# DeltaNet layer: meta-token products stacked in float32r, decay matrices against a constant operand, K's norms off a diagonal, and the last down pairs block by block

## Chip, cores and metric

The kernel runs on one core of a Trainium2 chip, as one launch. The metric is the device time of one execution in microseconds (us); lower is better. Engines: PE is TensorE (matmul), PEld its weight loads, DVE VectorE, ACT ScalarE, POOL GpSimd, SP SyncE. A "q" behind an engine's name is its instruction queue.

## The reference

A trunk of two layers over 16 learned meta tokens and 512 real tokens, of 1024 features: multi-scale retention, a SwiGLU feed-forward net (FFN), gated DeltaNet, a second FFN, and a last RMSNorm that drops the meta tokens. All in float32. The change lies in the DeltaNet layer and at the end of the last FFN. DeltaNet, cut to what matters (8 heads, keys of 128, values of 256; chunks of 64 with the meta tokens in a chunk of their own):

```python
qkv = silu(causal_conv(h @ w_qkv, conv_w));  beta = sigmoid(h @ w_beta)
g = -exp(a_log) * softplus(h @ w_a + dt_bias)
q = l2norm(q) * DK ** -0.5;  k = l2norm(k)          # l2norm: x * rsqrt(sum(x*x) + 1e-6)
def step(state, inp):                                # per chunk
    gam = cumsum(gc);  decay = exp(where(i >= j, gam_i - gam_j, -inf))
    a_mat = where(i > j, beta * (k @ k.T) * decay, 0)
    u, w = solve(eye + a_mat, [v * beta, k * beta * exp(gam)])
    v_new = u - w @ state
    o = (q * exp(gam)) @ state + ((q @ k.T) * decay) @ v_new
    state = state * exp(gam_last) + (k * exp(gam_last - gam)).T @ v_new
o = gated_head_norm(o, norm_w, gate) @ w_out
h = h + (silu(h @ w_gate) * (h @ w_up)) @ w_down     # the FFN behind it
```

## The kernel before

Tokens are kept as 16 + 512 columns (T = 528, two halves of HH = 264); the kernel works in chunks of 128 real tokens and one of the 16 meta tokens. A float32 product of the projections is done as three float32r products (`mm3`): both operands are split into a rounded part and the rest (`hi`, `lo`; `split`), and hi.hi, hi.lo and lo.hi are summed in PSUM. Weights come by DMA (`wraw`), ACT rounds them (`whi`, L171) and DVE makes the rest (`wlo`, L172); there are three buffers of whi and wlo. A few small products use plain float32; each of them is two matmul instructions in the profile. A gemm of a projection is 8 x 3 x 2 products of 264 columns into a PSUM tile `g` (two buffers); smaller products share four PSUM tiles `m`.

The stages of the DeltaNet layer: `dn_gates` computes beta and g (48 products of 16 rows, `wh`/`wl` as the fixed operand, tiles kh and kl), their cumulated sums, and for each head the decay matrix of its four chunks: DVE multiplies the constant mask `later` by g (L1173), PE multiplies that by `tri` (L1180), ACT takes the exponent (L1182), POOL masks it with `tri` (L1183), a DMA stores it in d_dec. `dn_keys` runs two gemms per head (K is s = 0, Q is s = 1): PSUM is scaled into `pad` by DVE (L1057), the convolution is one ACT and three DVE operations (L1060, L1062), then silu (L1065) and the split `z` (L404, L405). `dn_norms` transposes K or Q on PE (L1211) and sums squares on ACT with an accumulated output (L1215), for the meta tokens too (L1220, L1222). `dn_attention` makes cc = beta / (norm + eps) and two other factors from it on DVE and POOL, then K.[K Q] for each chunk (12 products of 256 columns), scales the result by cc and the decay (L1254), and does the meta tokens' K.K (L1266, L1267). `dn_inverse` inverts the 32x32 blocks of all heads at once on DVE; `dn_merge` builds larger blocks on PE (L1330, L1360); `dn_by_token` transposes V; `dn_states` scans over the chunks for two heads at a time, and begins with the meta tokens: um.v0 (L1416), then kw.(that) gives the first state (L1425). Then `ffn1`: its second half of the down projection sums 22 x 128 hidden rows into four PSUM tiles, one for a block of 128 tokens; only the last pair of weight tiles is done block by block, and `add`, sum of squares, power on POOL, scaling and output DMA of a block follow (L1660 to L1678).

What sets the order: these stages are generators that are advanced in turn while gemms run (`spawn`, `tick`, `finish`, with constants such as NORMS, ATTEND and HOP that say after how many steps one is due), and a scheduler that then orders each engine's instructions. An engine's queue is fixed and is run in order: an instruction that waits holds up all behind it.

Of the kernel before, what the change touches and what calls it, by code (L numbers as in the profile page):

```python
# [48 lines left out]
HOP = 1.6  # L49


class Hybrid:
# [1015 lines left out]
    def dn_gates(self, sp, x, rb):  # L1068
# [23 lines left out]
        ba = self.t(self.tp, [P, T], "ra", bufs=4)[:16]
        nc.vector.tensor_tensor(self.halves(ba), p[:16, :, :HH], self.halves(rb[:16, :]), op=ALU.mult)
        yield GATE_STEPS[0]
        pt = self.psum_m()
        for ch in range(5):
            c0 = 0 if ch == 0 else NM + (ch - 1) * P
            nc.tensor.transpose(pt[:, ch * 16 : ch * 16 + 16], ba[:, c0 : c0 + P], self.ident[:16, :16])
        bt = self.t(gp, [P, 5, 16], "bt_")
        nc.scalar.copy(bt, pt[:, :80].rearrange("p (a b) -> p a b", b=16))  # L1100
        S = [P, 5, DH]
        beta, ax = self.t(gp, S, "beta"), self.t(gp, S, "ax_")
# [37 lines left out]
        for dst, mat in ((self.eglast, self.ones), (self.ekw, self.later)):  # L1140
# [3 lines left out]
            mm(pg[:, :DH], mat[:NM, :], gf[:NM, :DH], start=True, stop=True)  # L1144
# [4 lines left out]
        glm = self.um  # L1149
        S = [NM, DH, NM]  # L1150
        nc.vector.tensor_tensor(
# [16 lines left out]
        )  # L1168
        for hd in range(DH):
            yield 1  # L1170
            pd = self.psum_m()
            gls = self.t(sp, [P, 4, P], "vs", bufs=4)
            nc.vector.tensor_tensor(  # L1173
                gls,
                self.later.unsqueeze(1).to_broadcast([P, 4, P]),
                g[:, 1:, hd : hd + 1].to_broadcast([P, 4, P]),
                op=ALU.mult,
            )
            for ch in range(4):
                nc.tensor.matmul(pd[:, ch * P : (ch + 1) * P], gls[:, ch, :], self.tri, start=True, stop=True)  # L1180
# [5 lines left out]
    def dn_keys(self, pool, hd, x, rb, first, gt):  # L1186
# [5 lines left out]
        for s, base in ((1, 0), (0, 8)):  # L1192
# [10 lines left out]
            norms.append(self.spawn(self.dn_norms(hd, s, t_), NORMS))  # L1203
        return self.spawn(self.dn_attention(pool, hd, zh, zl, norms, gt), ATTEND)

    def dn_norms(self, hd, s, t_):
        nc = self.nc
        ssk = self.ssk[:, hd, :]
        pt = self.psum_m()
        for c in range(4):  # L1210
            nc.tensor.transpose(pt[:, c * P : (c + 1) * P], t_[:, NM + c * P : NM + (c + 1) * P], self.ident)  # L1211
        for c in range(4):
            jk = self.t(self.sp, [P, P], "rh")
            dst = ssk[:, c + 1 : c + 2] if s == 0 else self.eq[:, hd, c : c + 1]
            nc.scalar.activation(jk, pt[:, c * P : (c + 1) * P], AF.Square, accum_out=dst)  # L1215
        if s == 0:
            nc.vector.tensor_copy(self.kmf[:, hd, :], t_[:, :NM])
            yield 1
            pt = self.psum_m()
# [595 lines left out]
```

## Time and profile before

| | us |
|---|---|
| median of three runs | 1714.14 (1713.79 to 1717.31) |
| the profiled execution, whole | 1718.1 |
| its span, first to last instruction | 1716.3 |
| PE, DVE, ACT, POOL busy | 1687.9, 1193.9, 854.8, 89.1 |
| mean granted clock of TensorE | 0.994 |
| gates | from 819 to 839.5 |
| decay matrices of the eight heads, and the first head's attention | from 839.5 to 859.5 |
| keys, norms and attention of the eight heads | from 859.5 to 954.5 |
| inverse | from 954.5 to 1021 |
| scans in four pairs | from 1021 to 1330 |
| second FFN and output | from 1330 on |

Each profile row of an engine gives start and duration in us, engine, line, operation, output<-inputs by the program's names, and the form. A matmul's duration is the time from its start to its modelled end; since matmuls are pipelined, the distance between two starts is what one costs. In brackets stands the idle time before, and what ended it. Rows of groups by line end in busy time, mean ns of one, and idle time before them.

### The profile page before, as it was taken

The page shows a single profiled execution, that of the slowest core. Times are in us where ns is not written, and L with a number is a line of the kernel's source. Part 1 is how long each engine was busy: PE and PEld are TensorE (multiplying, and loading weights), DVE is VectorE, ACT ScalarE, POOL GpSimd, SP SyncE. Part 2 cuts the span into 40 slices and gives each one's busy share as a digit, 9 for nine tenths or more (in the row PEclk, how much of TensorE's full clock was granted, in tenths as well). Part 3 has the DMA queues.
Part 4 walks back from the last instruction along what each step waited for, and adds up shares of the span by engine and source line. Part 5 has one row for each costly group of instructions (what it writes and reads, how often), then busy time and mean ns, then how long its engine had stood idle before and what let it go on. Part 6 is the DMA issues. An engine that isn't in the chain of part 4 may idle for free.

```text
span 1716.3 us, 30519 instructions
## 1 busy us (share of the span) xinstructions
PE 1687.9 (98%) x12455; PEld 1575.2 (92%) x12455; DVE 1193.9 (70%) x1848; ACT 854.8 (50%) x1532; POOL 89.1 (5%) x148
## 2 busy tenths in 40 slices
PE   9999999999999999999999999999999999999997
PEld 9999999999999999999899988797977889999886
DVE  7786877754698887433788767685858798887322
ACT  5445555532445555322665437675656554545322
POOL 1000000000000000000210001010101000000010
PEclk9999999999999999999999999999999999999999
DMA  5554746562223333323264472333322222333221
GB/s 205 161 168 117 214 109 191 173 212 87 100 85 105 105 99 93 92 91 98 99 207 156 130 208 67 124 104 108 106 100 73 96 88 99 102 108 109 88 99 49
DMA packets 87116, 207.16 MB, mean 121 GB/s; under 512 B 20176, under 2 KB 37760, under 8 KB 85696
## 3 DMA queue, kind: packets, MB, share of 16 engines
q1 hardware_dynamic: 77056, 193.13, 33.7%
q0 software_dynamic: 2960, 10.24, 3.4%
q10 hardware_dynamic: 6960, 1.84, 0.5%
q8 instruction: 98, 1.61, 0.4%
q14 instruction: 42, 0.34, 0.1%
HBM read 180.85 MB, written 24.33 MB: 120 GB/s over the span
## 4 chain that ended last, share of the span: by engine, by line
PE 69%; DVE 8%; issue 5%; ACT 2%; POOL 1%; DMA 0%; ACTq 0%; POOLq 0%; DVEq 0%
PE g L414 54%; PE m L414 11%; DVE wlo L405 1%; DVE ra L1062 1%; DVE wlo L172 1%; DVE wsum L212 1%; POOL ss L1475 0%; ACT whi L404 0%; DVE flt L405 0%; PE m L1211 0%; PE m L1387 0%; DVE flb L405 0%; DMA wraw<-in_w_ret_dram 0%; ACT whi L171 0%; PE m L1330 0%
## 5 line engine op out<-in xcount | busy, mean ns | idle before, releaser
L172 DVE TENSOR_TENSOR wlo<-wraw,whi 128x1024 fp32r<-128x1024 f32 (+1 forms) x140 | 166.3, 1190 | 182.7 <-ACT whi L171 180.7
L171 ACT CAST whi<-wraw 128x1024 fp32r<-128x1024 f32 (+1 forms) x140 | 143.3, 1024 | 274.1 <-PE g L414 155.1
L414 PE MATMUL g<-xhi,whi 128*128 128x264 f32 (+1 forms) x1024 | 255.6, 314 | 2.5 <-DVE ra L775 2.4
L414 PE MATMUL g<-fht,whi 128*128 128x264 f32 (+1 forms) x912 | 256.6, 286 | 0.0
L414 PE MATMUL g<-fht,wlo 128*128 128x264 f32 (+1 forms) x912 | 254.9, 284 | 0.8 <-DVE wlo L405 0.8
L414 PE MATMUL g<-flt,whi 128*128 128x264 f32 (+1 forms) x912 | 254.4, 283 | 0.0
L414 PE MATMUL g<-xhi,wlo 128*128 128x264 f32 (+1 forms) x1024 | 249.9, 309 | 2.0 <-DVE wlo L172 2.0
L414 PE MATMUL g<-xlo,whi 128*128 128x264 f32 (+1 forms) x1024 | 249.3, 308 | 0.3 <-DVE xlo L468 0.3
L404 ACT CAST whi<-wraw 128x1024 fp32r<-128x1024 f32 x129 | 135.5, 1051 | 127.8 <-issue 51.3
L405 DVE TENSOR_TENSOR wlo<-wraw,whi 128x1024 fp32r<-128x1024 f32 x129 | 157.3, 1220 | 32.2 <-ACT whi L404 31.6
L414 PEld LDWEIGHTS g<-xhi,whi 128*128 128x128 f32 x1024 | 167.9, 191 | 12.6 <-DVE ra L775 2.6
L414 PEld LDWEIGHTS g<-xhi,wlo 128*128 128x128 f32 x1024 | 167.9, 191 | 10.7 <-DVE wlo L172 2.2
L414 PEld LDWEIGHTS g<-xlo,whi 128*128 128x128 f32 x1024 | 167.6, 190 | 7.4 <-DVE xlo L468 0.7
L414 PEld LDWEIGHTS g<-flt,whi 128*128 128x128 f32 x912 | 170.7, 189 | 0.2
L414 PEld LDWEIGHTS g<-fht,wlo 128*128 128x128 f32 x912 | 169.7, 188 | 1.0 <-DVE wlo L405 1.0
L414 PEld LDWEIGHTS g<-fht,whi 128*128 128x128 f32 x912 | 170.1, 188 | 0.4 <-ACT whi L404 0.2
L414 PE MATMUL g<-fhb,whi 128*128 128x264 f32 (+1 forms) x480 | 134.1, 288 | 0.0
L414 PE MATMUL g<-fhb,wlo 128*128 128x264 f32 (+1 forms) x480 | 132.6, 284 | 0.6 <-DVE wlo L405 0.5
L414 PE MATMUL g<-flb,whi 128*128 128x264 f32 (+1 forms) x480 | 132.0, 283 | 0.0
L405 DVE TENSOR_TENSOR wlo<-wsum,whi 128x1024 fp32r<-128x1024 f32 x54 | 66.1, 1225 | 44.3 <-ACT whi L404 44.3
L414 PEld LDWEIGHTS g<-fhb,wlo 128*128 128x128 f32 x480 | 88.5, 188 | 1.0 <-DVE wlo L405 1.0
L414 PEld LDWEIGHTS g<-flb,whi 128*128 128x128 f32 x480 | 89.1, 189 | 0.1
(445 smaller groups left out, 3769.9 us busy)
## 6 DMA issues: line engine op xcount, KB each, us to landing
wraw<-in_w_gu_dram SPq DMA_DIRECT2D x66, 512.0 KB, 3.2
wraw<-in_w_ret_dram SPq DMA_DIRECT2D x56, 512.0 KB, 4.1
wraw<-in_w_d_dram SPq DMA_DIRECT2D x38, 512.0 KB, 3.4
sraw<-in_w_gu_dram SPq DMA_DIRECT2D x22, 512.0 KB, 3.5
wraw<-in_w_ret_dram POOLq DMA_DIRECT2D x18, 512.0 KB, 5.5
wraw<-in_w_ro_dram SPq DMA_DIRECT2D x16, 512.0 KB, 3.5
wraw<-in_w_dqk_dram SPq DMA_DIRECT2D x16, 512.0 KB, 3.3
wraw<-in_w_dv_dram SPq DMA_DIRECT2D x16, 512.0 KB, 4.1
```

What stands on the lines that cost most here:

```text
L171: nc.scalar.copy(hi[:, c], raw[:, c])
L172: nc.vector.tensor_tensor(lo[:, c], raw[:, c], hi[:, c].bitcast(F32), op=ALU.subtract)
L212: nc.vector.scalar_tensor_tensor(dst[:, k, :], hh[:, kb + k, cs], g[:, kb + k : kb + k + 1], rb[:, cs], op0=ALU.mult, op1=ALU.mult)
L404: self.nc.scalar.copy(hi, src)
L405: self.nc.vector.tensor_tensor(lo, src, hi.bitcast(F32), op=ALU.subtract)
L414: mm(o, l, r[which], start=first and n == 0, stop=last and n == 2, **kw)
L1062: nc.vector.scalar_tensor_tensor(acc, pad[:, i : i + T], cw[:, mt, i : i + 1], acc, op0=ALU.mult, op1=ALU.add)
```

## The change

Line numbers in this section are those of the changed kernel.

**Gates.** hi and lo of w_ba lie in one fixed operand of 48 columns (rows 0 to 15 and 32 to 47 of the result), so two products with x's hi and lo replace three, 32 in place of 48. The five transposes become products against `pick`, which also adds the two parts. The meta tokens' values are spread to three copies, 32 rows apart.

**Decay matrices.** The mask `tri` is multiplied by g's hi and lo parts (two DVE products per head, L1194) and the constant `after` is the fixed operand of two 512-wide float32r products (L1200), where before four 128x128 float32 products had `tri` as the other operand.

**K's norms.** `dn_norms` is left for Q alone. For K, `diagonal` takes the sums of squares from the diagonal of K.K, which attention makes anyway: DVE multiplies a 128x128 block in PSUM by the identity and writes the accumulated sum (L1257), five times per head (one block of 96x96 for the meta tokens). cc and what follows come only after them, so the PSUM tiles of both chunk pairs and of the meta tokens are held until then.

**Meta products.** For um.v0 and kw.wm the meta tokens stand three times, 32 rows apart, as hi, hi and lo of one operand against hi, lo and hi of the other, so that one float32r product of 96 rows gives the three terms (L1461, L1474); DVE spreads and subtracts (L1464, L1469, L1418), and um is loaded by three DMAs and split (L1345).

**Tail.** `LAST = 2`: in the second half the last two pairs of down weights are held and done block by block.

The diff, cut to what the text speaks of:

```diff
+        wst = self.t(sp, [P, KT, 48], "zl", F32R, bufs=3)
+        nc.gpsimd.memset(wst.bitcast(F32), 0.0)
+        self.split(wst[:, :, 0:16], wst[:, :, 32:48], wr)
...
+            for i in range(2):
+                for half in range(2):
+                    nc.tensor.matmul(
+                        p[:48, half, :HH],
+                        wst[:, kt, :],
+                        x[i][:, kt, half * HH : half * HH + HH],
+                        start=kt == 0 and i == 0,
+                        stop=kt == KT - 1 and i == 1,
+                    )
...
+        after = self.t(sp, [P, P], "kh", F32R)
+        nc.scalar.copy(after, self.later)
+        g2 = self.t(sp, [P, 2, n5], "kl", F32R)
+        self.split(g2[:, 0, :], g2[:, 1, :], gf)
+        g2 = g2.rearrange("p t (a b) -> p t a b", b=DH).bitcast(F32)
...
-            gls = self.t(sp, [P, 4, P], "vs", bufs=4)
-            nc.vector.tensor_tensor(
-                gls,
...
-            )
-            for ch in range(4):
-                nc.tensor.matmul(pd[:, ch * P : (ch + 1) * P], gls[:, ch, :], self.tri, start=True, stop=True)
+            upto = self.t(sp, [P, 2, 4, P], "vs", F32R, bufs=4)
+            for i in range(2):
+                nc.vector.tensor_tensor(
+                    upto[:, i],
+                    self.tri.unsqueeze(1).to_broadcast([P, 4, P]),
+                    g2[:, i, 1:, hd : hd + 1].to_broadcast([P, 4, P]),
+                    op=ALU.mult,
+                )
+                nc.tensor.matmul(pd, after, upto[:, i].rearrange("p a b -> p (a b)"), start=i == 0, stop=i == 1)
...
-            norms.append(self.spawn(self.dn_norms(hd, s, t_), NORMS))
+            if s == 0:
+                nc.vector.tensor_copy(self.kmf[:, hd, :], t_[:, :NM])
+            else:
+                norms.append(self.spawn(self.dn_norms(hd, t_), NORMS))
...
+        def diagonal(dst, ps):
+            n = ps.shape[1]
+            jk = self.t(self.sp, [P, P], "rh")
+            nc.vector.scalar_tensor_tensor(
+                jk[:n, :n], ps, 1.0, self.ident[:n, :n], op0=ALU.mult, op1=ALU.mult, accum_out=dst
+            )
+
+        pk = self.psum_m()
+        self.spread(self.km, self.kmf[:, hd, :])
+        nc.tensor.matmul(pk[:96, :96], self.km, self.km, start=True, stop=True)
+        diagonal(ssk[:96, 0:1], pk[:96, :96])
+        ps = []
...
+                diagonal(ssk[:, c + 1 : c + 2], ps[cp][:, ci * 256 : ci * 256 + P])
+        nc.vector.tensor_scalar(irk, ssk, EPS, None, op0=ALU.add)
+        nc.vector.reciprocal(cc, irk)
+        nc.vector.tensor_tensor(cc, cc, self.beta[:, :, hd], op=ALU.mult)
+        for c in range(4):
...
-        km = self.kmf[:, hd, :]
-        nc.tensor.matmul(ps[:NM, :NM], km, km, start=True, stop=True)
         nc.vector.scalar_tensor_tensor(
-            self.mtm[:, hd, :], ps[:NM, :NM], cc[:NM, 0:1], self.decm0[:, hd, :], op0=ALU.mult, op1=ALU.mult
+            self.decm0[:, hd, :], pk[:NM, :NM], cc[:NM, 0:1], self.decm0[:, hd, :], op0=ALU.mult, op1=ALU.mult
...
+        for b in range(3):
+            (nc.sync, nc.scalar)[b % 2].dma_start(um[32 * b : 32 * b + NM], self.d_m1)
+        nc.scalar.copy(self.um, um)
+        nc.vector.tensor_tensor(self.um[64:96], um[64:96], self.um[64:96].bitcast(F32), op=ALU.subtract)
...
+        v0 = self.t(sp, [96, 256], "v0", F32R, bufs=4)
         irk = self.irk[:, hd, :]
+        vm = self.vm
+        for i in range(2):
+            self.spread(vm[:, i, :], va[i][:, :NM])
...
+        nc.vector.scalar_tensor_tensor(
+            v0[32:64], pt[32:64, :256], irk[32:64, 0:1], v0[32:64].bitcast(F32), op0=ALU.mult, op1=ALU.subtract
+        )
...
+        u3 = self.u3[hd % 2]
+        self.spread(u3, self.um[:, hd, :])
+        self.spread(self.km, self.kmf[:, hd, :])
         ps = self.psum_m()
-        mm(ps[:NM, :256], self.um[:, hd, :], vs[:NM, 0, :], start=True, stop=True)
-        wm = self.t(sp, [P, 256], "rr")
-        nc.scalar.copy(wm[:NM, :], ps[:NM, :256])
-        ps = self.psum_m()
-        nc.tensor.transpose(ps[:NM, :P], self.kmf[:, hd, :], self.ident)
-        kw = self.t(sp, [P, P], "kwf")
-        nc.scalar.activation(kw[:NM, :], ps[:NM, :P], AF.Copy, scale=self.kws[:NM, hd, 0:1])
+        mm(ps[:96, :256], u3, v0, start=True, stop=True)
+        wm = self.t(sp, [P, 256], "rh", F32R)
+        nc.scalar.copy(wm[:96], ps[:96, :256])
+        nc.vector.tensor_tensor(wm[32:64], ps[32:64, :256], wm[32:64].bitcast(F32), op=ALU.subtract)
...
+        nc.vector.scalar_tensor_tensor(
+            kw[64:96], kt_[64:96], kws[64:96], kw[64:96].bitcast(F32), op0=ALU.mult, op1=ALU.subtract
+        )
         yield
         ps = self.psum_m()
-        mm(ps[:, :256], kw[:NM, :], wm[:NM, :], start=True, stop=True)
+        mm(ps[:, :256], kw[:96], wm[:96], start=True, stop=True)
...
+            held = []
+            apart = LAST if half else 1
...
+                held.append((kp, self.load_w(a["w_d1"][half, kp])))
+                steps = [(k, i, b, w) for k, w in held for i in range(2) for b in range(4)]
+                if kp >= FT // 2 - apart:
+                    if len(held) < apart:
+                        continue
+                    steps.sort(key=lambda s: s[2])
+                held = []
+                for k, i, b, w in steps:
+                    kt, bs = 2 * k + i, slice(b * P, (b + 1) * P)
...
```

Where it moves instructions, at three places.

PE, decay burst, before. The tiles m are PSUM, one for each head, vs the products of L1173; g_9615 is a gemm of the key phase. The heads stand in one piece (the eighth follows):

```order
L414 MATMUL g_9615<-xhi_7750,whi_9611 128x264
L1160 MATMUL m_9426<-tri_471,um_9035 16x16 x8
L1180 MATMUL m_9437<-tri_471,vs_9438 128x128 x4
L1180 MATMUL m_9448<-tri_471,vs_9449 128x128 x4
L1180 MATMUL m_9459<-tri_471,vs_9460 128x128 x4
L1180 MATMUL m_9470<-tri_471,vs_9471 128x128 x4
L1180 MATMUL m_9481<-tri_471,vs_9482 128x128 x4
L1180 MATMUL m_9492<-tri_471,vs_9493 128x128 x4
L1180 MATMUL m_9503<-tri_471,vs_9504 128x128 x4
```

PE at the same place, after (kh is the constant `after`, vs one product of L1194; g_9604 and g_9685 are gemms, whi and wlo their weights):

```order
L1200 MATMUL m_9426<-vs_9427,kh_9421 128x512
L415 MATMUL g_9604<-xhi_7750,whi_9600 128x264
L415 MATMUL g_9604<-xlo_7751,whi_9600 128x264 x2
L1200 MATMUL m_9426<-vs_9427,kh_9421 128x512
L415 MATMUL g_9604<-xhi_7750,wlo_9601 128x264 x2
L415 MATMUL g_9685<-xhi_7750,whi_9681 128x264
L1200 MATMUL m_9436<-vs_9437,kh_9421 128x512
L415 MATMUL g_9685<-xhi_7750,whi_9681 128x264
L415 MATMUL g_9685<-xlo_7751,whi_9681 128x264 x2
L1200 MATMUL m_9436<-vs_9437,kh_9421 128x512
```

The products of the eight heads no longer stand together: up to the last of the sixteen, two rows with three gemm products lie between two of them.

DVE, key phase, before. The gemms' PSUM tiles follow each other on PE as g_9615, g_9695, g_9812, g_9892; pad takes one out, wlo_9889 is a weight tile of g_9892:

```order
L1057 TENSOR_TENSOR pad_9677<-g_9615,rb_9155 128x528
L172 TENSOR_TENSOR wlo_9889<-wraw_9886,whi_9888 128x1024
L1062 SCALAR_TENSOR_TENSOR ra_9680<-pad_9677,convw_475,ra_9680 128x528 x2
L1231 TENSOR_SCALAR irk_9030<-ssk_9027 128x5
L1062 SCALAR_TENSOR_TENSOR ra_9680<-pad_9677,convw_475,ra_9680 128x528
L1232 RECIPROCAL cc_9028<-irk_9030 128x5
L1233 TENSOR_TENSOR cc_9028<-cc_9028,beta_9290 128x5
L1234 TENSOR_TENSOR kws_9029<-cc_9028,ekw_9323 128x5
L1254 SCALAR_TENSOR_TENSOR vs_9734<-m_9741,cc_9028,zh_9732 128x256 x2
```

DVE, a little later in the key phase, after. Here the gemms are g_9795, g_9876, g_9986, and wlo_9983 belongs to g_9986; L1257 are the diagonals:

```order
L1058 TENSOR_TENSOR pad_9858<-g_9795,rb_9162 128x528
L556 COPY km_9035<-kmf_9033 128x3x16
L173 TENSOR_TENSOR wlo_9983<-wraw_9980,whi_9982 128x1024
L1063 SCALAR_TENSOR_TENSOR ra_9861<-pad_9858,convw_475,ra_9861 128x528
L1257 SCALAR_TENSOR_TENSOR rh_9895,ssk_9027<-m_9892,ident_113 96x96
L1063 SCALAR_TENSOR_TENSOR ra_9861<-pad_9858,convw_475,ra_9861 128x528
L1257 SCALAR_TENSOR_TENSOR rh_9910,ssk_9027<-m_9903,ident_113 128x128
L1063 SCALAR_TENSOR_TENSOR ra_9861<-pad_9858,convw_475,ra_9861 128x528
L1257 SCALAR_TENSOR_TENSOR rh_9912,ssk_9027<-m_9903,ident_113 128x128
L1257 SCALAR_TENSOR_TENSOR rh_9927,ssk_9027<-m_9920,ident_113 128x128
L1257 SCALAR_TENSOR_TENSOR rh_9929,ssk_9027<-m_9920,ident_113 128x128
```

Before, the wlo behind a gemm's pad belongs to the third gemm after it, with two gemms between; after, to the second, with one between. In the decay burst, after, the sixteen products of L1194 stand back to back on DVE, and the wlo of g_9795 comes only after them and seven further rows.

DVE, the end of the program, before (xhi is the residual, m_18305 to m_18308 the four blocks' sums, fr the norm's factor, fnw the norm's weight):

```order
L1660 TENSOR_TENSOR xhi_17903<-xhi_17903,m_18305 128x512
L1660 TENSOR_TENSOR xhi_17903<-xhi_17903,m_18306 128x512
L1670 SCALAR_TENSOR_TENSOR fr_18642<-fss_17904 128x1
L1677 SCALAR_TENSOR_TENSOR xhi_17903<-xhi_17903,fr_18642,fnw_17867 128x512
L1670 SCALAR_TENSOR_TENSOR fr_18652<-fss_17904 128x1
L1660 TENSOR_TENSOR xhi_17903<-xhi_17903,m_18307 128x512
L1677 SCALAR_TENSOR_TENSOR xhi_17903<-xhi_17903,fr_18652,fnw_17867 128x512
L1660 TENSOR_TENSOR xhi_17903<-xhi_17903,m_18308 128x512
L1670 SCALAR_TENSOR_TENSOR fr_18662<-fss_17904 128x1
L1677 SCALAR_TENSOR_TENSOR xhi_17903<-xhi_17903,fr_18662,fnw_17867 128x512
```

DVE, the end of the program, after (the blocks' sums are m_18313 to m_18316):

```order
L1716 TENSOR_TENSOR xhi_17911<-xhi_17911,m_18313 128x512
L1726 SCALAR_TENSOR_TENSOR fr_18650<-fss_17912 128x1
L1733 SCALAR_TENSOR_TENSOR xhi_17911<-xhi_17911,fr_18650,fnw_17875 128x512
L1716 TENSOR_TENSOR xhi_17911<-xhi_17911,m_18314 128x512
L1726 SCALAR_TENSOR_TENSOR fr_18660<-fss_17912 128x1
L1733 SCALAR_TENSOR_TENSOR xhi_17911<-xhi_17911,fr_18660,fnw_17875 128x512
L1716 TENSOR_TENSOR xhi_17911<-xhi_17911,m_18315 128x512
```

Before, the second block is added ahead of the first one's scaling, the fourth ahead of the third's. After, each block is added, normed and scaled in turn; on PE each block's sum has twelve products in a row at its end, from whi_18589 and whi_18595, where it had six.

More of the change, by code (lines that the diff above doesn't have):

```diff
@@ L1096, in dn_gates @@
         for ch in range(5):
[L1097 to L1100, printed above, removed]
+            src = bm[:48] if ch == 0 else ba[:, NM + (ch - 1) * P : NM + ch * P]
+            n = src.shape[1]
+            nc.tensor.matmul(pt[:n, ch * 16 : ch * 16 + 16], src, pick, start=True, stop=True)
+        tmp = self.t(sp, [P, 4 * P], "zh", bufs=3)
+        bt = tmp[:, :80].rearrange("p (a b) -> p a b", b=16)
+        ax, xa, e, z, z2, q = (
+            tmp[:, 80 + 40 * i : 120 + 40 * i].rearrange("p (a b) -> p a b", b=DH) for i in range(6)
+        )
+        nc.gpsimd.memset(bt[:, 0, :], 0.0)
+        nc.scalar.copy(bt[:96, 0, :], pt[:96, :16])
+        nc.scalar.copy(bt[:, 1:, :], pt[:, 16:80].rearrange("p (a b) -> p a b", b=16))
         S = [P, 5, DH]
-        beta, ax = self.t(gp, S, "beta"), self.t(gp, S, "ax_")
+        beta = self.t(gp, S, "beta")
         nc.scalar.activation(beta, bt[:, :, :DH], AF.Exp, scale=-1.0)
@@ L1139, in dn_gates @@
         nc.vector.tensor_scalar(self.ngam, self.egam, -1.0, None, op0=ALU.mult)
-        for dst, mat in ((self.eglast, self.ones), (self.ekw, self.later)):
+        later3 = self.t(sp, [NM, P], "oq")
+        nc.gpsimd.memset(later3, 0.0)
+        self.spread(later3[:, :96], self.later[:NM, :NM])
+        for dst, mat, meta in ((self.eglast, self.ones, self.ones[:NM, :]), (self.ekw, self.later, later3)):
             pg = self.psum_m()
@@ L1143, in dn_gates @@
             df = dst.rearrange("p a b -> p (a b)")
-            mm(pg[:, :DH], mat[:NM, :], gf[:NM, :DH], start=True, stop=True)
+            mm(pg[:, :DH], meta, gf[:NM, :DH], start=True, stop=True)
             mm(pg[:, DH:n5], mat, gf[:, DH:], start=True, stop=True)
@@ L1229, in dn_attention @@
         ssk = self.ssk[:, hd, :]
[L1230 to L1236 removed]
+        cc, kws, irk = self.cc[:, hd, :], self.kws[:, hd, :], self.irk[:, hd, :]
         dec = self.t(pool, [P, 4, P], "zh", bufs=3)
@@ L1632, in ffn1 @@
             hs = slice(half * 512, half * 512 + 512)
+            held = []
+            apart = LAST if half else 1
             for kp in range(FT // 2):
-                w = self.load_w(a["w_d1"][half, kp])
-                last = kp == FT // 2 - 1
-                order = [(i, b) for i in range(2) for b in range(4)]
-                if last:
-                    order = [(i, b) for b in range(4) for i in range(2)]
-                for i, b in order:
-                    kt = 2 * kp + i
-                    bs = slice(b * P, (b + 1) * P)
+                held.append((kp, self.load_w(a["w_d1"][half, kp])))
[7 more added lines that the diff above has]
+                    kt, bs = 2 * k + i, slice(b * P, (b + 1) * P)
                     self.mm3(
```

115 lines of the change are left out of this document (51 added, 64 removed).

## The prediction

> **What bounds the kernel now.** I read the page's busy shares and its chain first, then cut the span into stages by windows, then went through the stages that the change touches.
>
> ```profile
> span 1716.3 us, 30519 instructions
> PE 1687.9 (98%) x12455; PEld 1575.2 (92%) x12455; DVE 1193.9 (70%) x1848; ACT 854.8 (50%) x1532; POOL 89.1 (5%) x148
> PE 69%; DVE 8%; issue 5%; ACT 2%; POOL 1%; DMA 0%; ACTq 0%; POOLq 0%; DVEq 0%
> ```
>
> TensorE is busy 98% of the span and carries most of the chain of waits. So a matmul taken away is worth its time wherever no other engine is about to run out, and that depends on the stage. The windows give, after start:end, the length and the busy time of PE, PE's weight loads, DVE, ACT and POOL, then clock, DMA share and GB/s:
>
> ```profile
> 819.00:839.50 20.50, 20.16 (x165) 18.37 (x163) 17.47 (x39) 14.11 (x19) 0.31 (x3) 1.00 0.33 106
> 839.50:859.50 20.00, 16.77 (x146) 15.76 (x146) 17.41 (x26) 13.06 (x37) 10.61 (x9) 1.00 0.34 118
> 859.50:954.50 95.00, 95.00 (x784) 93.60 (x783) 78.83 (x155) 58.44 (x180) 11.96 (x22) 1.00 0.53 175
> 1021.00:1082.00 61.00, 58.14 (x465) 51.41 (x464) 44.25 (x92) 40.49 (x108) 7.43 (x14) 0.93 0.36 118
> 1082.00:1330.00 248.00, 244.60 (x1681) 199.47 (x1680) 171.85 (x316) 156.94 (x364) 16.53 (x34) 0.99 0.30 99
> ```
>
> They are gates, decay burst, key phase, the first scan pair and the later ones. In the key phase PE has no gap; DVE is at 83%. Over the first three windows (135.5 us) PE works 131.9 us and DVE 113.7, so DVE has 21.8 us left. Each edit here takes time from PE and three of them give some to DVE: that balance decides the case.
>
> **Gates.** The 48 products are 264 wide.
>
> ```profile
> 822.89 0.40 PE L414 MATMUL g<-xhi,kh 128*16 128x264 f32 x2
> ...
> 828.43 0.40 PE L414 MATMUL g<-xhi,kl 128*16 128x264 f32 x2
> ```
>
> 46 of them take 5.54 us from start to start, 0.12 each. Sixteen go: -1.9. Five transposes become five products against `pick`, the same count; the spread, the memsets and the two small copies are on engines with room in this window. I allow 0.3 for their chain: -1.6 on PE, bounds -1.9 and 0.
>
> **Decay matrices.** Before, one DVE product per head feeds eight short matmuls; after, two DVE products feed two of 512 columns.
>
> ```profile
> 844.01 6.72 PE L1180 MATMUL m<-tri,vs 128*128 128x128 f32 x56
> 852.97 1.13 PE L1180 MATMUL m<-tri,vs 128*128 128x128 f32 x8 [2.23 <-DVE vs L1173]
> L1173 DVE TENSOR_TENSOR vs<-later,g__01342_9318 x8: 672/682/1761, 840.2 to 851.1; 128x512 f32<-128x512 f32 x8
> L1183 POOL TENSOR_TENSOR zl<-zl,tri x8: 1266/1616/1749, 845.9 to 860.5; 128x512 f32<-128x512 f32 x8
> L1173 DVE TENSOR_TENSOR vs<-later,g__01342_9318 128x512 f32<-128x512 f32 x8 | 8.4, 1070 | 1.8 <-PE m L1180 1.8
> ```
>
> PE: 64 x 0.12 = 7.7 us go. A 512-wide product costs 0.235, from two neighbours in the tail (both started with no gap):
>
> ```profile
> 1702.45 0.39 PE L414 MATMUL m<-whi,hidpl 128*128 128x512 f32 x1
> 1702.68 0.40 PE L414 MATMUL m<-whi,hidph 128*128 128x512 f32 x1
> ```
>
> Sixteen of them are 3.8 us, so PE saves 3.9. DVE gains eight 128x512 products: 5.4 us at 0.67, 8.6 at the mean of 1.07. The mean is high because a product that runs beside POOL's L1183 takes as long as POOL does (up to 1.76 beside 1.75); POOL's eight multiplications stay. The order puts all 16 products in one piece on DVE, so that the next wlo and the pad that PE wants stand behind them; PE has about three gemm products between two L1200, 16 x (0.235 + 3 x 0.12) = 9.5 us of work against 10.7 to 17.1 on DVE. The 2.23 us wait of PE on this product therefore does not go away, it is spread out.
>
> The Trainium skill ("SBUF — State Buffer", "SBUF: two separate sides") calls this an exclusive lock, held for a whole instruction between GpSimd and a DVE operation with two SBUF inputs. The trace agrees: 0.67 us alone, 1.76 beside POOL's 1.75. By that rule each of POOL's eight products holds up one DVE product, before as after, so the contested share would not double; the sum would use 5.4 and not 8.6.
>
> **K's norms.** For each head four PE transposes go, and one of 16 rows for the meta tokens.
>
> ```profile
> 841.06 0.63 PE L1211 MATMUL m<-ident,ra 128*128 128x128 f32 x4
> 841.45 0.37 PE L414 MATMUL g<-xhi,whi 128*128 128x264 f32 x1
> L1215 ACT ACTIVATION_READ_ACCUMULATOR rh<-m x64: 194/206/221, 841.9 to 951.6; 128x1 f32 x64
> L1456 DVE SCALAR_TENSOR_TENSOR kl<-m,kws,kh 128x128 fp32r<-128x128 f32 x6 | 2.1, 351 | 0.9 <-ACT kh L1455 0.8
> ```
>
> The four take 0.39, the fifth a quarter of that, and the meta product of 96 columns in place of 16 gives that back: 8 x 0.39 = 3.1 off PE. ACT loses five squares per head and is not the bound (58.44 of 95). DVE gets 40 diagonals with an accumulated output. The trace has none on DVE. The nearest row is the 128x128 product of L1456, 0.35 us as busy time; back to back it may be 0.28. Whether the accumulated sum is read by a second instruction is not to be seen on DVE; on ACT it is, 0.206 us each. So 40 x 0.28 = 11.2 at the least, 40 x (0.35 + 0.206) = 22.2 at the most; I take 16, nearer to the bare product, since the ends of ACT's reads overlap with the next square. Spreading km adds 8 x 0.175 = 1.4 (row of the kmf copy, below). No DVE work goes.
>
> The Trainium skill ("VectorE: DVE Perf Modes", "Two Vector instructions with no wait between them") says that an operation that also writes out its accumulator is two instructions, the main one and an accumulator read. No DVE row here shows it. By it the upper half of the range holds.
>
> DVE's balance for 819 to 954.5: 113.7 + (5.4 to 8.6) + (11.2 to 22.2) + 1.4 = 131.7 to 146; with 6.6, 16 and 1.4 it is 137.7. PE would need 131.9 - 1.6 - 3.9 - 3.1 = 123.3. At every value DVE is above PE, so none of PE's 8.6 us can be cashed in full here: DVE becomes the bound. What DVE waits for today inside the key phase:
>
> ```profile
> L405 DVE TENSOR_TENSOR z<-ra,z 128x512 fp32r<-128x512 f32 x13 | 9.2, 705 | 2.9 <-ACT z L404 2.9
> L1057 DVE TENSOR_TENSOR pad<-g,rb 128x528 f32<-128x528 f32 x13 | 9.1, 702 | 6.1 <-PE g L414 6.1
> L1217 DVE COPY kmf<-ra 128x16 f32<-128x16 f32 x6 | 1.0, 175 | 4.3 <-ACT ra L1065 4.3
> ```
>
> The 6.1 on PE's g vanishes when DVE is late; the 7.2 on ACT can be filled, since the diagonals stand in the queue there. I take DVE without a gap, 137.7: +2.2 against 135.5 now. The bounds are -8.6 (PE's sum) and +10.5 (146). Who waits is PE: in the order a wlo now stands behind diagonals and about one gemm ahead of its use, where it stood two ahead.
>
> **Meta products in the scan.** For a head, um by v0 and kw by wm are fp32 with two passes each; two heads stand here:
>
> ```profile
> 1033.10 0.60 PE L1416 MATMUL m<-vs,um 16*16 16x256 f32 x2
> 1033.63 0.28 PE L1420 MATMUL m<-ident,kmf 128*16 128x128 f32 x1
> ...
> 1034.94 1.20 PE L1425 MATMUL m<-rr,kwf 16*128 16x256 f32 x4
> 1036.07 0.59 PE L414 MATMUL g<-xhi,wlo 128*128 128x264 f32 x1
> ```
>
> 0.53 + 1.13 / 2 = 1.10 becomes two products at 0.12: -0.86, for eight heads -6.9 at most. DVE gets, per head, two spreads of v, one of u and of km (4 x 0.175) and three subtractions (about 0.35 each): 1.75 us, 14 in all. DVE is at 73% in the first pair's window and 69% in the later ones, so a good part fits, but each subtraction lies on the chain to the first state (copy, subtract, product, copy, subtract) and makes it some 0.7 us longer. Pair 0 has the fewest gemms to cover it; pairs 2 and 3 keep their order. I take half, -3.5, bounds -6.9 and 0. The inverse's um now arrives by three DMAs, a copy and a subtraction; its first product stands 12 us into the scan's window, and that is the cover (0.4 us of DVE and the DMAs' latency if it were gone).
>
> **Tail.** Two pairs at once give each block 12 x 0.235 = 2.82 us of PE, where it had 1.41.
>
> ```profile
> 1702.88 0.69 DVE L1660 TENSOR_TENSOR xhi<-xhi,m 128x512 f32<-128x512 f32 x1 [10.34 <-PE m L414]
> ...
> 1704.14 0.18 ACT L1662 ACTIVATION_READ_ACCUMULATOR fj<-xhi 128x1 f32 x1
> ...
> 1706.67 0.40 PE L414 MATMUL m<-whi,hidpl 128*128 128x512 f32 x1
> ...
> 1707.25 0.75 DVE L1677 SCALAR_TENSOR_TENSOR xhi<-xhi,fr,fnw 128x512 f32<-128x512 f32 x1
> 1707.92 0.68 DVE L1660 TENSOR_TENSOR xhi<-xhi,m 128x512 f32<-128x512 f32 x1
> ...
> 1708.98 0.19 ACT L1662 ACTIVATION_READ_ACCUMULATOR fj<-xhi 128x1 f32 x1
> ...
> 1709.44 0.54 POOL L1673 TENSOR_TENSOR fr<-fr,mhalf 128x1 f32<-128x1 f32 x1 [2.22 <-DVE fr L1670]
> ...
> 1710.01 0.75 DVE L1677 SCALAR_TENSOR_TENSOR xhi<-xhi,fr,fnw 128x512 f32<-128x512 f32 x1 [0.65 <-POOL fr L1673]
> 1710.79 0.34 ACTq L1678 DMA_DIRECT2D out_dram<-xhi  x1
> ...
> 1712.27 0.35 ACTq L1678 DMA_DIRECT2D out_dram<-xhi  x1
> ```
>
> Today the last output leaves 5.60 us after the last matmul starts, since DVE has two blocks in hand. One block alone: add to read 1.26, read to power 0.46, to scaling 0.57, to its DMA 0.78: 3.07. DVE can add again 2.29 + 0.67 = 2.96 after the last add, 0.14 over PE's 2.82, so 0.42 is lost over three blocks. From the last matmul: 0.43 to its add, 0.42, 3.07 = 3.9, or -1.7; I take -1.6, bounds -2 and -0.7.
>
> **Sum.** +2.2 (gates, decay and norms together) - 3.5 - 1.6 = -2.9. The profiled run took 1718.1 for its span of 1716.3; the sum gives 1715.2 on that scale. It stands 4.0 over the median of 1714.14, so on the median's scale it is 1711.
>
> **Rivals.** *PE's time shows* (DVE reorders its idle time well, and the diagonals cost 0.28 or less): -8.6 - 6.9 - 1.6 = -17, half of that more likely than all: 1697 to 1705. For it: PE is the bound today. Against: DVE's balance. *DVE bound on the upper side*: if the accumulator read costs 0.2, 40 of them and full diagonals make +10.5 in the key phase, with -5.1 after it: +5.4, 1719.5, slower. It decides where DVE's work in these windows passes 144 us: +8.5, which the 5.1 after it turns into the smallest loss that can be told. For it: 0.206 on ACT, and L1173's 1.07 beside POOL. Against: the inverse after it has some gemm cover that could take a late DVE in. *The scan gives nothing*: its chain grows by as much as PE saves; +2.2 - 1.6 = +0.6, 1714.7, no change.
>
> **Chances.** A difference under 0.2% (3.4 us, so 1710.7 to 1717.6) cannot be told from no change. The sum as forecast 0.50, spread 1706 to 1716, so 0.26 faster, 0.22 same, 0.02 slower; PE's time shows 0.15, faster; upper DVE bound 0.27, slower; scan nothing 0.08 (0.06 same, 0.02 slower). Faster 0.41, same 0.28, slower 0.31. The range leaves out the far half of the first rival and the end of the second: 1700 to 1721.
>
> **What would show it.** DVE's busy share from 819 to the last diagonal above 95%, and PE gaps put down to DVE wlo or DVE vs; diagonal rows of 0.28 to 0.35, with or without a read beside each; 16 L1200 at 0.235; L1461 and L1474 at 0.12; the last output under 4.1 us after the last matmul's start. I am wrong if the key phase gets shorter with DVE under 90%, or if PE stalls in pair 0's scan by more than 3.5 us over now.

## The result and the profile after

The changed kernel takes 1704.51 us in the median (1702.91 to 1707.59, four runs), the kernel before 1715.14 (1713.79 to 1717.31). The ratio is 0.9939, 95% interval 0.9921 to 0.9957: 10.6 us faster. The direction and the range of the prediction held; the sum behind its 1711 did not: it had 2.9 us.

The head of the page of the changed kernel, as the one shown of before:

```profile
span 1702.4 us, 30391 instructions
PE 1672.2 (98%) x12340; PEld 1565.0 (92%) x12340; DVE 1212.1 (71%) x2006; ACT 843.5 (50%) x1456; POOL 97.2 (6%) x157
PE 81%; DVE 9%; issue 5%; ACT 3%; DMA 1%; POOL 1%; SPq 0%; POOLq 0%; ACTq 0%; DVEq 0%
```

PE lost 15.7 us of busy time and 13.9 us of span. To leave out the untouched first part (1.4 us of that difference lie before the first gates product), one window goes from the first gates product to the last matmul, in the kernel before and in the changed one (start:end, length, then busy PE, PEld, DVE, ACT, POOL):

```profile
822.89:1706.67 883.78, 870.82 (x5914) 767.66 (x5914) 623.60 (x1059) 470.11 (x973) 55.08 (x91) 0.99 0.34 110
```
```profile
821.51:1694.50 872.99, 855.80 (x5799) 758.34 (x5799) 641.84 (x1217) 459.46 (x899) 62.80 (x95) 0.99 0.35 113
```

PE is busy 15.0 us less and idle 4.2 us more (17.2 against 13.0): -10.8. Another 1.5 came at the tail. The two profiles differ by more than the medians (13.9 against 10.6 us), since the profiled execution of the kernel before, 1718.1, lies 3 us over its median. So most of the matmul time that the change removes showed, and the question is why DVE, which got 18 us more to do, did not take it.

What DVE does for a diagonal: start, duration, the last two of one head.

```profile
948.83 0.29 DVE L1257 SCALAR_TENSOR_TENSOR rh<-m,ident 128x128 f32<-128x128 f32 x1
949.05 0.08 DVE L1257 DVE_READ_ACCUMULATOR rh<-m,ident 128x1 f32 x1
949.05 0.29 DVE L1257 SCALAR_TENSOR_TENSOR rh<-m,ident 128x128 f32<-128x128 f32 x1
949.26 0.09 DVE L1257 DVE_READ_ACCUMULATOR rh<-m,ident 128x1 f32 x1
```

The accumulated sum is read by a second instruction, as the Trainium skill says ("VectorE: DVE Perf Modes", "Two Vector instructions with no wait between them"), but that one starts with the next product beside it. From product to product it is 0.21 to 0.22 us in all.

The decay burst and the key phase by windows, and then the burst's lines (count, min/median/max ns, first and last start):

```profile
838.40:859.50 21.10, 16.39 (x120) 14.75 (x120) 14.12 (x30) 12.24 (x27) 11.64 (x7) 0.92 0.17 60
859.50:947.20 87.70, 87.08 (x701) 86.06 (x700) 83.41 (x230) 46.72 (x109) 17.58 (x23) 0.98 0.60 198
```
```profile
L1194 DVE TENSOR_TENSOR vs<-tri,kl x16: 671/672/674, 843.1 to 852.2; 128x512 fp32r<-128x512 f32 x16
```
```profile
L1203 POOL TENSOR_TENSOR zl<-zl,tri x8: 1251/1281/6777, 847.8 to 864.6; 128x512 f32<-128x512 f32 x8
```

In the key phase DVE is at 95%, and PE still idles only 0.6 of 87.7 us. In the burst none of DVE's products is held up any more (before, up to 1.76 us); instead one of POOL's mask products takes 6.8 us: it starts at 847.8, and DVE's products run on to 852.9. What that does to PE, by its waits and ACT's, and along the timeline:

```profile
PE m L1200 <- ACT zl L1202: 4.2, 1, 4.2
```
```profile
ACT zl L1202 <- DMA d_dec<-zl: 7.8, 3, 6.6
```
```profile
847.79 9.22 POOL L1203 TENSOR_TENSOR zl<-zl,tri 128x512 f32<-128x512 f32 x3 [6.07 <-ACT zl L1202]
...
854.59 2.76 SPq L1204 DMA_DIRECT2D d_dec<-zl  x3
856.70 0.60 ACT L1202 ACTIVATE zl<-m 128x512 f32<-128x512 f32 x1 [6.56 <-DMA d_dec<-zl]
857.35 0.79 PE L1200 MATMUL m<-vs,kh 128*128 128x512 f32 x1 [4.22 <-ACT zl L1202]
```

The late mask delays the store to d_dec, the store holds one of three tiles zl, the exponent waits for the tile, the PSUM tile stays full, and PE stops for 4.2 us. From 1.4 us before the end of that stop the granted clock is halved (the third figure from the end of this window; PE works 4.9 of its 6.8 us, so that 2.5 us are lost):

```profile
855.90:862.70 6.80, 4.93 (x19) 4.23 (x20) 2.49 (x10) 3.12 (x5) 4.95 (x5) 0.50 0.79 282
```

The tail: the last matmul, the last add, the last output.

```profile
1694.45 0.40 PE L415 MATMUL m<-whi,hidpl 128*128 128x512 f32 x1
...
1695.46 0.68 DVE L1716 TENSOR_TENSOR xhi<-xhi,m 128x512 f32<-128x512 f32 x1
...
1698.59 0.34 ACTq L1734 DMA_DIRECT2D out_dram<-xhi  x1
```

4.14 us where it had been 5.60.

### The profile page after: what moved, and what is told of

It reads as the page before. It is cut to its first block, busy times and chain, and to the rows that moved or that the text cites. A ratio compares the mean times of both kernels' runs of the same rounds, so it can differ in the third digit from the quotient of the medians.

```text
span 1702.4 us, 30391 instructions
## 1 busy us (share of the span) xinstructions
PE 1672.2 (98%) x12340; PEld 1565.0 (92%) x12340; DVE 1212.1 (71%) x2006; ACT 843.5 (50%) x1456; POOL 97.2 (6%) x157
## 4 chain that ended last, share of the span: by engine, by line
PE 81%; DVE 9%; issue 5%; ACT 3%; DMA 1%; POOL 1%; SPq 0%; POOLq 0%; ACTq 0%; DVEq 0%
PE g L415 63%; PE m L415 14%; DVE wlo L406 1%; DVE wlo L173 1%; POOL zl L1203 1%; DVE wsum L213 1%; ACT whi L405 0%; DVE flt L406 0%; PE m L513 0%; DVE flb L406 0%; DMA rr<-d_m 0%; PE m L499 0%; ACT whi L172 0%; DVE ra L1063 0%; POOL ss L1524 0%
## 5 line engine op out<-in xcount | busy, mean ns | idle before, releaser
L415 PEld LDWEIGHTS g<-xhi,wlo 128*128 128x128 f32 x1024 | 166.9, 189 | 10.2 <-DVE wlo L173 2.2
L415 PEld LDWEIGHTS g<-fhb,whi 128*128 128x128 f32 x480 | 89.1, 189 | 0.1
```

The costliest lines, as they stand in the source:

```text
L415: mm(o, l, r[which], start=first and n == 0, stop=last and n == 2, **kw)
```

## The experiments

Two theories go into them. Theory 1: the matmul time that is removed shows, less new stops, since DVE's new work is cheaper than the prediction took it. Theory 2, the prediction's: DVE takes the key phase's saving away. There are twelve kernels, in three batches beside the kernel before. Batch one takes parts of the change out again.

> The changed kernel again, as the yardstick for the runs beside it: about 1704.5 us, 10 to 11 under the kernel before. Both theories say the same here.

Measured: 1705.02 us, ratio 0.9944 (0.9932 to 0.9955). A ratio here is known to 0.0009 to 0.0017, 2 to 3 us, so that differences of 2 to 3 us between two variants are on the edge of what times can tell. Where they don't, the traces are compared by the table below.

**K's norms back** (`norms`):

```diff
-            if s == 0:
-                nc.vector.tensor_copy(self.kmf[:, hd, :], t_[:, :NM])
-            else:
-                norms.append(self.spawn(self.dn_norms(hd, t_), NORMS))
+            norms.append(self.spawn(self.dn_norms(hd, s, t_), NORMS))
...
-                diagonal(ssk[:, c + 1 : c + 2], ps[cp][:, ci * 256 : ci * 256 + P])
```

> The changed kernel with K's norms as they were: transposes on PE, squares with an accumulated sum on ACT, no diagonal on DVE (the meta tokens' part in 96 rows). Theory 1 (the matmul time that is removed shows almost in full, since a diagonal with its read costs DVE only 0.21 us): 8 x 0.39 us come back, so about 3 us over the changed kernel. Theory 2 (that of the prediction: DVE takes the key phase's saving away): no loss, or up to 3 us faster, since 8.4 us of DVE work leave.

Measured: 1706.74 us, 0.9956 (0.9943 to 0.9969); 1.7 us over the changed kernel in the medians, intervals overlapping. By time alone neither theory is settled; `maskn` below asks it again. The order of this kernel also has a stop of 3.7 us in the inverse, at 1011, where ACT's rounding of a weight is late; the changed kernel has one of 1.4 us there. So the 1.7 us are not the norms alone.

**Decay matrices back** (`decay`):

```diff
-            upto = self.t(sp, [P, 2, 4, P], "vs", F32R, bufs=4)
...
+            gls = self.t(sp, [P, 4, P], "vs", bufs=4)
...
+            for ch in range(4):
+                nc.tensor.matmul(pd[:, ch * P : (ch + 1) * P], gls[:, ch, :], self.tri, start=True, stop=True)
```

> The changed kernel with the decay matrices as they were: one DVE product and four 128x128 matmuls per head. Theory 1: 3.9 us of matmuls come back, and the new wait of 4.2 us behind POOL's mask product goes while one of 2.2 comes back: about 2 us over the changed kernel. Theory 2: no loss or up to 3 us faster, since 5.4 us of DVE work leave.

Measured: 1706.53 us, 0.9958 (0.9943 to 0.9974); 1.5 us over, as theory 1 has it, but inside the interval. In its profile the stop of 4.2 us is gone, with the half clock behind it, and three stops of 1.0 to 1.6 stand in its place.

**One pair at the end** (`last1`):

```diff
-LAST = 2
+LAST = 1
```

> The changed kernel with only the last down pair block by block, as before. Both theories: 1.5 us over the changed kernel, and in its profile the last output leaves 5.6 us after the last matmul's start, where the changed kernel has about 4. Were it 0, the end would be bound by the output's DMA.

Measured: 1705.24 us, 0.9951 (0.9936 to 0.9966); the times don't separate it. The profile does: 5.61 us from the last matmul's start to the last output, against 4.14 and 4.13 in the two profiles of the changed kernel.

Batch two. **Mask on PE** (`mask`):

```diff
+                nc.tensor.matmul(
+                    pd[:, i * 256 : i * 256 + 256], eye, never.rearrange("p a b -> p (a b)"), start=False, stop=i == 1
+                )
...
-            nc.gpsimd.tensor_tensor(de, de, self.tri.unsqueeze(1).to_broadcast([P, 4, P]), op=ALU.mult)
```

> The changed kernel with POOL's eight mask products taken away: before the exponent PE adds a constant of 0 or -1024 to the sums (two products of 256 columns per head against the identity). In the changed kernel PE stands still 4.2 us at 853 because the exponent waits for a tile whose mask product on POOL took 6.8 us while DVE made its sixteen products back to back; behind the stop the clock is halved for 6.8 us. Theory 1 (POOL, held off by DVE, makes that stop): the stop and the half clock go (-4.6 and -3.4 at most), 1.9 us of products come: 3 to 6 us under the changed kernel, no gap over 1 us on PE from 850 to 860. Rival (the tiles wait for their DMA to d_dec anyhow): the gap stays at 3 us or more, and it is 0 to 2 us slower.

Measured: 1697.04 us, 0.9899 (0.9882 to 0.9916): 7 to 8 us under the changed kernel, more than expected. The profiled execution is the slowest of the four (1702.95, the others 1696.09 to 1697.54): 10.2 us at half clock, from 1022.2 on, stand in it. The burst has no gap left:

```profile
840.00:859.50 19.50, 19.48 (x156) 18.46 (x157) 17.94 (x43) 15.27 (x38) 0.30 (x2) 1.00 0.47 161
```

That POOL's mask product is what stops PE is shown by this; whether DVE's stream is what holds POOL off is asked by `psumtri`.

**Meta products of the scan back** (`scan`): the two products in plain float32 on 16 rows.

```diff
-        mm(ps[:96, :256], u3, v0, start=True, stop=True)
+        mm(ps[:NM, :256], self.um[:, hd, :], v0, start=True, stop=True)
...
-        mm(ps[:, :256], kw[:96], wm[:96], start=True, stop=True)
+        mm(ps[:, :256], kw[:NM, :], wm[:NM, :], start=True, stop=True)
```

> The changed kernel with the meta tokens' products of the scan as they were (plain float32, 16 rows; um by one DMA; no spreads and subtractions). Theory 1 (PE's time shows, less what the longer chain costs in idle time): 4 to 7 us over the changed kernel, PE's gaps in the first pair's scan fall back to about 7.5 us for all scans. Theory 2 (half of it, the prediction): 3.5 us over it. Rival (the longer chain eats it): no difference.

Measured: 1708.43 us, 0.9960 (0.9947 to 0.9972), 3.4 over: half of the 6.9, as the prediction took it. The intervals overlap, so by times alone the rival is not excluded; the table below has the work that comes back.

**Gates back** (`gates`): 48 products of 16 rows.

```diff
-                        wst[:, kt, :],
...
+            self.mm3(
+                [p[:16, 0, :HH], p[:16, 1, :HH]],
```

> The changed kernel with the 48 products of 16 rows for beta and g in place of the 32 stacked ones. Theory 1: 1.9 us of matmuls come back and nothing else: 2 us over the changed kernel (1.6 by the prediction). Rival (the stage is bound by DVE's chain of small operations): no difference.

Measured: 1707.66 us, 0.9959 (0.9945 to 0.9973), 2.6 over, intervals overlapping. By place it is 1.9: the 768th gemm product of 264 columns behind the first gates product, near the end of the attention, starts 132.5 us after it, in the changed kernel 130.7.

**Diagonals twice** (`diag2`):

```diff
+            for _ in range(2):
+                jk = self.t(self.sp, [P, P], "rh")
+                nc.vector.scalar_tensor_tensor(
```

> The changed kernel with each diagonal taken twice, 40 more DVE operations with their reads, 8.4 us at 0.21 each; the result is the same. It asks where DVE becomes the bound of the key phase, where it was busy 83.4 of 87.7 us. Theory 1 (DVE still has room there, 4.3 us, and PE a lead of 46 gemm products): 2 to 5 us over the changed kernel, with DVE at 97% or more in the key phase. Theory 2 (DVE is the bound already): 8 us over it. Rival (DVE's idle time is anywhere when needed): under 1 us.

Measured: 1715.39 us, 1.0001 (0.9992 to 1.0010): all of the change's gain is gone, 10.4 us by the medians for 8.4 to 8.8 us of DVE work. DVE is at 96% of the key phase, and PE waits:

```profile
859.50:950.00 90.50, 87.23 (x702) 85.96 (x702) 86.57 (x297) 45.15 (x108) 17.38 (x23) 0.99 0.54 179
```
```profile
PE g L415 <- ACT whi L172: 3.7, 1, 3.7
PE g L415 <- DVE pad L1058: 2.1, 1, 2.1
```

The 3.7 lie in the inverse, at 1023. A wait like it is in `norms` and in `maskn`, which have less DVE work, so DVE's load is not shown to make it; the pad's wait of 2.1 lies in the key phase and is DVE's. Idle time is 21.9 us in this profile (16.3 and 17.2 in the two of the changed kernel), and 9.9 us are lost to half clock (10.0 and 5.9). Up to the 768th gemm product of 264 columns, near the end of the attention, this kernel needs 133.44 us from the first gates product, the changed one 130.65: 2.8 us for the 40 more diagonals. Most of the rest is the stop in the inverse and half clock. So 40 more make a wait in the key phase that the change's 40 don't make; that DVE's load brings the whole 10.4 us is not shown.

Batch three. **The mask operand in PSUM** (`psumtri`):

```diff
+        tri = self.psum_m()
+        nc.scalar.copy(tri[:, :P], self.tri)
...
-                    self.tri.unsqueeze(1).to_broadcast([P, 4, P]),
+                    tri[:, :P].unsqueeze(1).to_broadcast([P, 4, P]),
```

> The changed kernel, but the sixteen DVE products of the decay matrices read their mask from a PSUM tile (one copy of it there by ACT), so that each has one input in SBUF and not two; POOL's mask products stay. Theory 1 (POOL was held off because DVE's back-to-back products took the SBUF access that POOL needs): POOL's first product takes about 1.3 us instead of 6.8, PE's stop at 853 falls under 1.5 us and the half clock behind it goes: 4 to 8 us under the changed kernel. Rival (three zl tiles and their DMA make the stop, POOL's 6.8 us is only how its span is recorded): the stop stays at 4 us, no difference.

Measured: 1705.88 us, 0.9948 (0.9936 to 0.9961): no difference. The cause was right and the gain was not:

```profile
L1205 POOL TENSOR_TENSOR zl<-zl,tri x8: 1282/1293/1305, 846.5 to 857.2; 128x512 f32<-128x512 f32 x8
```
```profile
L1196 DVE TENSOR_TENSOR vs<-m,kl x16: 667/668/672, 842.6 to 851.6; 128x512 fp32r<-128x512 f32 x16
```
```profile
PE g L415 <- DVE wlo L173: 1.6, 1, 1.6
PE m L415 <- DVE vs L1287: 1.5, 1, 1.5
PE m L1265 <- ACT rh L1240: 1.1, 1, 1.1
PE m L415 <- ACT zl L1204: 0.7, 1, 0.7
```

With one input of DVE's products in PSUM, POOL's eight take 1.29 us each and DVE's 0.67, side by side: DVE's stream with two SBUF inputs had held POOL off. That is the lock of the Trainium skill ("SBUF — State Buffer", "Who interferes with whom"), and the trace agrees with its condition of two inputs in SBUF. But the one stop of 4.2 us became four of 0.7 to 1.6, 4.9 in all, and 3.4 us of half clock stay there (6.8 before). The constant's tile takes one of the four PSUM tiles m for the burst, and the wlo behind the sixteen products is late, as the prediction had feared. Which of the two weighs more was not tried.

**Mask on PE, three pairs at the end** (`mask3`, the edit of `mask` and this):

```diff
-LAST = 2
+LAST = 3
```

> The version with the mask added on PE, and the last three down pairs block by block instead of two. The mask version again, 1697 us; by the prediction's tail (DVE's cycle of 2.96 us per block now under PE's 4.2) the 0.42 us lost over three blocks goes too: the last output 3.5 us after the last matmul's start, where two pairs give 4.13. Rival: the third pair's weights come too late and PE waits before the first block, up to 2 us slower.

Measured: 1698.05 us, 0.9901 (0.9887 to 0.9914); the times don't tell it from `mask`. The last output leaves 3.57 us after the last matmul's start:

```profile
1686.79 0.40 PE L415 MATMUL m<-whi,hidpl 128*128 128x512 f32 x1
...
1690.36 0.34 ACTq L1743 DMA_DIRECT2D out_dram<-xhi  x1
```

**Mask on PE, K's norms back** (`maskn`, the edits of `mask` and `norms` together):

> The version with the mask added on PE, with K's norms back on PE and ACT. It asks what the diagonals are worth where the stop in the decay burst is gone. Theory 1 (PE's time shows): 3 us over the mask version's 1697. Theory 2 (DVE is on the edge, so its 10 us weigh as much as PE's 3): no difference, within 1.5 us.

Measured: 1701.63 us, 0.9923 (0.9911 to 0.9936), 3.6 to 4.6 over the two versions with the mask. This is nearer to theory 1, though the intervals just touch. PE's work rises by 2.3 to 4.0 us over the three other versions with the mask (table below), which fits the 3.1 us of matmuls. It is not the whole difference: the order of this kernel too has the late rounding in the inverse, a stop of 3.4 us at 1008 with 6.8 us of half clock, where `mask` stops for 1.4.

**Spreads on POOL** (`maskp`, `mask3` and this, for km, v and um):

```diff
-        self.spread(self.km, self.kmf[:, hd, :])
+        self.spread(self.km, self.kmf[:, hd, :], nc.gpsimd)
```

> The version with the mask added on PE and three pairs at the end, with the spreads of km, v and um to three copies moved from DVE to POOL, which has nothing else there now: 40 copies of about 0.18 us leave DVE, 7 us. If DVE's load is what costs, 1 to 3 us under the version with three pairs. Rival (POOL's copies wait behind DVE's stream as its mask products did, and km is late for K.K): slower, up to 5 us, with PE waits for km or m behind L1263's line.

Measured: 1699.81 us, 0.9923 (0.9909 to 0.9936): not faster than `mask3`, 1.8 over it in the medians, intervals overlapping. The rival's wait is there: POOL's copy takes 0.65 us in the mean, where DVE's took 0.18, and

```profile
PE m L1272 <- POOL km L556: 1.1, 3, 0.6
```

One table holds the profiles together: the window from the first gates product to the last matmul, PE's busy time in it, what half clock cost (PE's busy time in the stretches that the trace's clock records hold at 0.50, halved), busy less lost, and idle. The fourth column is PE's work at full clock. The five kernels whose matmuls are the same (after, after2, last1, diag2, psumtri) have 849.1 to 850.9, so a difference of work is known to about 1 us each way.

| kernel | length | PE busy | lost to half clock | work | idle |
|---|---|---|---|---|---|
| before | 883.8 | 870.8 | 6.8 | 864.0 | 13.0 |
| after | 872.9 | 855.8 | 5.9 | 849.9 | 17.2 |
| after2 | 875.4 | 859.1 | 10.0 | 849.1 | 16.3 |
| norms | 874.1 | 859.2 | 7.1 | 852.0 | 15.0 |
| decay | 872.9 | 857.3 | 3.4 | 853.9 | 15.6 |
| last1 | 870.0 | 853.1 | 2.2 | 850.9 | 16.9 |
| scan | 876.5 | 861.5 | 5.7 | 855.8 | 15.0 |
| gates | 873.1 | 856.5 | 4.3 | 852.3 | 16.6 |
| diag2 | 882.0 | 860.1 | 9.9 | 850.2 | 21.9 |
| psumtri | 872.9 | 857.3 | 6.5 | 850.8 | 15.6 |
| mask | 870.1 | 857.7 | 6.8 | 850.9 | 12.4 |
| mask3 | 864.9 | 853.4 | 1.6 | 851.9 | 11.5 |
| maskn | 868.1 | 858.0 | 3.1 | 854.9 | 10.0 |
| maskp | 866.0 | 852.6 | 0.0 | 852.6 | 13.5 |

Undone one by one, the parts bring back 2.4 (gates), 4.0 (decay), 2.1 (norms) and 5.9 us (scan) of PE's work: 14.4, and the kernel before has 14.1 more. What goes the other way is idle time, 4.2 us more in the first profile of the changed kernel and 3.3 in the second. What is lost to half clock varies between executions of one kernel as well (5.9 and 10.0 in the two of the changed kernel), so one profile can't tell differences of that size.

## Why the prediction was right or wrong

**Direction and range: right, by another case than the one taken as likeliest.** 1704.5 is outside the spread that the forecast sum had (1706 to 1716) and inside that of the rival "PE's time shows" (0.15; 1697 to 1705), at its upper end: the matmul time showed, less 4.2 us of new idle time. The case taken, "DVE becomes the bound" in the key windows, did not happen. That the direction held is therefore luck as far as these windows go: their term was forecast as a loss, and the gain of the sum came from the scan and the tail alone.

**The step that failed** is "At every value DVE is above PE", and the term it gave, +2.2 for gates, decay and norms together. The same piece of work in the kernel before, the changed one, `mask` and `diag2`, from the first gates product to the 768th gemm product of 264 columns behind it, by which the attention of the eight heads is over (in `diag2` that of seven); start:end, length, then busy PE, PEld, DVE, ACT, POOL:

```profile
822.89:958.72 135.83, 132.31 (x1095) 128.30 (x1096) 112.79 (x218) 84.47 (x232) 22.88 (x33) 1.00 0.48 159
821.51:952.16 130.65, 125.28 (x996) 122.23 (x996) 116.49 (x318) 71.48 (x153) 30.92 (x35) 0.97 0.49 161
823.09:947.24 124.15, 123.90 (x1012) 121.89 (x1012) 115.36 (x318) 70.54 (x153) 14.20 (x27) 1.00 0.52 170
821.24:954.68 133.44, 125.40 (x995) 121.93 (x996) 119.58 (x378) 70.46 (x154) 29.85 (x34) 0.97 0.46 154
```

These stages took 5.2 us less, not 2.2 more, and 11.7 less once the stop is gone; there PE runs without a gap (123.9 of 124.2 us) and DVE, at 115.4 us, is below it. DVE's busy time rose by 3.7 us, where the prediction had 24.0 (6.6, 16 and 1.4). Its lower end was not a lower end.

Forty diagonals were put at 11.2 to 22.2 us, with 16 taken; they cost 40 x 0.22 = 8.8 at most. The nearest row's duration (0.35) and a guess of 0.28 stood for the price, where a diagonal is 0.28 long and the next starts 0.21 to 0.22 behind it, and the read of the sum was priced with ACT's 0.206, where DVE's is 0.08 and hidden. The decay products were put at 6.6; the sixteen take 9.7 us where the eight took 8.4, which is 1.3 more, since the time that POOL had held those eight up stood already in the 113.7. With these two the balance is 113.7 + 1.3 + 8.8 + 1.4 = 125.2: still above the 123.3 that PE would need, so these prices alone don't turn it. For the rest, the rows that stood there already came to some 8 us less: one wlo falls out of the window, and rows that follow each other at once overlap at their ends, as the diagonals' rows show; how the 8 us split is not worked out. `diag2` doesn't rescue the step: with up to 40 diagonals more DVE is busy 119.6 of 133.4 us, and the stages are still 2.4 us shorter than before.

Of the signs that the prediction named, the diagonals' 0.28 with a read beside each came true. DVE's share from 819 to the last diagonal, above 95% by the forecast, was 89% (116.3 of 130.3 us), and PE's waits on DVE's wlo and vs come to 0.6 us in the key phase.

**Matmul terms: right within what the table can tell.** 1.9, 3.9, 3.1 and 6.9 us were to go from PE, 15.8 in all; 14.1 went (the split between parts by undoing is 2.4, 4.0, 2.1 and 5.9; what undoing one part moves in the order of the others is in these).

**Decay: the wait is spread, but by another engine.** The prediction had the contested access stay with DVE, "up to 1.76 beside 1.75", and the wlo behind the sixteen products late. None of DVE's sixteen was held up. In a row without a pause DVE kept POOL out instead, and the price came through POOL, the store and the exponent: a stop of 4.2 us and a half clock behind it. That path was not in the prediction, which followed DVE's and PE's queues only and costed POOL's eight products as unchanged. The late wlo is real, but it was behind this stop and showed once POOL was free (`psumtri`).

**Gates** (-1.6): 2.6 by the medians, 2.4 by work, 1.9 by place. **Scan** (-3.5, half): 3.4 by the medians. Its work is 5.9 and idle time is 1.3 to 2.2 us lower without it, so by the table the longer chain takes a fifth to two fifths, not half; the difference lies within the interval. **Tail** (-1.6, to 3.9 us): 4.14, that is -1.47. The cycle of 2.96 us on DVE that was set against PE's 2.82 was 3.0 (1692.45 to 1695.46); with 4.2 us of PE per block (`mask3`) it is hidden.

**Norms**: no gain was predicted beside DVE's load. In the changed kernel the gain can't be told from none by times (1.7 us); without the stop it is 3.6 to 4.6. By work it is 2.1 beside the stop and 2.3 to 4.0 without, so whether it is worth less beside the stop is open.

## What to carry to other kernels

Before a cheap engine is declared the bound, its unit price must come from start-to-start distances: a diagonal's row is 0.28 us long and the next starts 0.22 behind it, and the prediction took 0.40 for each of forty. Busy time also holds what another engine held up, so a product that is added to such rows must not be priced at their mean. Where two engines' sums of busy time come within a few per cent of each other, a sum alone did not say here which one waits. When an engine's queue gets a long piece without a pause, look at what shares SBUF access with it, and follow that engine's output to whoever waits; here taking eight products from POOL and adding 1.9 us to PE won another 7 to 8 us, to 0.9899 of the kernel before (0.9882 to 0.9916).

## What was not expected of the hardware

An accumulated sum on DVE costs next to nothing where products follow each other: 0.08 us of read that overlaps, 0.21 to 0.22 from product to product. DVE's products with two SBUF inputs, sixteen in a row, let POOL in at no point between them: 6.8 us for a product of 1.28, while DVE ran at 0.67 each; with one of DVE's inputs in PSUM both ran at their own pace (`psumtri`). In the kernel before, where DVE's eight were not in one piece, it was DVE that was held up, to 1.76.

The stops of PE had a second price: 6.8 us of half clock at the stop of 4.2 to 4.4, with 4.4 to 6.3 us of PE's work in it, so 2.2 to 3.1 lost, in all of the seven profiles that have this stop (the changed kernel twice, `norms`, `last1`, `scan`, `gates`, `diag2`), and none at that place in the four with the mask on PE. Shorter stops don't tell: one of 1.96 us had 6.8 us of half clock behind it (the kernel before, from 1018.8), two of 1.45 and 0.87 had 10.2 (`mask`, from 1022.2), and one of 2.23 had none (the kernel before, at 851).
